# Copying each row in 16 column blocks, one for each DMA engine, with the first 128 columns apart

## The chip, the cores and the metric

One core of a Trainium2 chip. The metric is the device time of one execution in microseconds (us); lower is better. GB/s in the profiles is what the copies moved one way; read plus written is twice that. A run counts as "slow" here if it is over 1.5% above the fastest run of the same kernel, and verdicts use the other runs ("fast") alone. Several chips of the same kind were used, so a kernel is compared with the kernel before *on the same chip*; absolute times from different jobs are not compared.

## The reference

```python
def setup_inputs():
    return {"x": np.random.randn(8192, 8192).astype(np.float32), "shift": 100}

def reference(x, shift):
    return np.roll(x, shift, axis=1)
```

Each row of 8,192 floats (32 KiB) is rotated right by 100 columns (400 B). Nothing is computed. 268 MB are read and 268 MB written.

## The kernel before

```python
    s = shift % n_cols                      # 100
    engines = [nc.sync, nc.scalar]          # two queues that issue transfers
    n_chunks = 16
    rows_per_chunk = n_rows // n_chunks     # 512

    for i in range(n_chunks):
        r0 = i * rows_per_chunk
        r1 = r0 + rows_per_chunk
        eng = engines[i % 2]
        eng.dma_start(out=out[r0:r1, s:], in_=x[r0:r1, : n_cols - s])    # the wide copy
        eng.dma_start(out=out[r0:r1, :s], in_=x[r0:r1, n_cols - s:])     # the narrow copy
# ... launch code cut
```

Every copy goes from HBM to HBM, with no stop on the core. Below, "wide copy" and "narrow copy" are the two kinds marked here; a "packet" is one contiguous run of bytes, as the trace records it.

## Time and profile before

| | before |
|---|---|
| time, 3 runs | 850.75 us (848.87 to 853.41) |
| span of the profile | 830.1 us |
| packets of 32,368 B (wide) | 8,192, mean 1,568 ns, fastest tenth 1,199 ns |
| packets of 400 B (narrow) | 8,192, mean 35 ns, median 24 ns |

The profiled execution was about 20 us shorter than the three timed ones. In the other runs below, the span is only about 2 us under the time of the same run, and this kernel took 836 to 842 us on other chips. So this profile seems to come from a faster chip, and a difference between it and another profile has to be taken with that in mind.

From the page of the kernel before: the span; the mean busy share of the 16 DMA engines in 40 equal slices of the span, in tenths; what they moved in each slice; packet counts; the two queues with packets, MB and share of the 16 engines' span; and HBM traffic.

```profile
span 830.1 us, 77 instructions
...
DMA  9999999999999999999999999999999999999996
GB/s 306 324 326 315 328 322 323 331 329 328 334 323 334 338 311 340 324 334 334 306 339 324 332 329 314 328 331 335 329 305 335 332 328 326 311 334 328 329 326 208
DMA packets 16896, 268.44 MB, mean 323 GB/s; under 512 B 8704, under 2 KB 8704, under 8 KB 8704
...
q1 hardware_dynamic: 8448, 134.22, 49.8%
q10 hardware_dynamic: 8448, 134.22, 49.1%
HBM read 268.44 MB, written 268.44 MB: 647 GB/s over the span
```

The engines are busy in every slice but the last. 49.8% and 49.1% for the two queues mean that packets fill nearly all of the engines' time. The HBM line (HBM is the chip's main memory) is the limit to look at: 647 GB/s of reads and writes. The Trainium skill (HBM Reference, Specifications) gives about 716 GB/s for the memory that two cores share; the trace is at 90% of that. That the memory is what limits the kernel is the reading that fits.

The next lines are the order of issues around the end of a chunk: start, duration (both us), the queue, line, operation, and how many were merged. L33 is the wide copy, L34 the narrow one.

```profile
start us, us, engine line op out<-in xcount [idle before <-releaser]
311.49 0.51 SPq L33 DMA_DIRECT2D out_dram<-in_x_dram  x1
313.59 0.52 ACTq L33 DMA_DIRECT2D out_dram<-in_x_dram  x1
315.96 94.76 SPq L34 DMA_DIRECT2D out_dram<-in_x_dram  x1
317.51 93.26 ACTq L34 DMA_DIRECT2D out_dram<-in_x_dram  x1
```

A wide copy is issued in 0.5 us. The narrow copy behind it is held up for 93 to 95 us, because the queue takes no more for the time being; by then the next wide copy is already in the queue. The same place in a table of windows (window in us, POOL, clock, busy share of the DMA engines, GB/s); 300 to 320 us is where the narrow packets run:

```profile
core 0: us, POOL busy (x), PEclk, DMA share, GB/s
250.00:300.00 50.00, 0.00 (x0) 1.00 0.99 333
300.00:320.00 20.00, 0.00 (x0) 1.00 0.99 307
320.00:370.00 50.00, 0.00 (x0) 1.00 1.00 334
```

The engines stay busy there, at 307 in place of 333 GB/s.

### The profile page before, as it was taken

The page shows a single profiled execution, that of the slowest core. Times are in us where ns is not written, and L with a number is a line of the kernel's source. Part 1 is how long each engine was busy: PE and PEld are TensorE (multiplying, and loading weights), DVE is VectorE, ACT ScalarE, POOL GpSimd, SP SyncE. Part 2 cuts the span into 40 slices and gives each one's busy share as a digit, 9 for nine tenths or more (in the row PEclk, how much of TensorE's full clock was granted, in tenths as well). Part 3 has the DMA queues.
Part 4 walks back from the last instruction along what each step waited for, and adds up shares of the span by engine and source line. Part 5 has one row for each costly group of instructions (what it writes and reads, how often), then busy time and mean ns, then how long its engine had stood idle before and what let it go on. Part 6 is the DMA issues. An engine that isn't in the chain of part 4 may idle for free. (4 is left out here: it accounts for less than half of the span.)

```text
span 830.1 us, 77 instructions
## 1 busy us (share of the span) xinstructions
POOL 0.2 (0%) x4
## 2 busy tenths in 40 slices
POOL 0000000000000000000000000000000000000000
DMA  9999999999999999999999999999999999999996
GB/s 306 324 326 315 328 322 323 331 329 328 334 323 334 338 311 340 324 334 334 306 339 324 332 329 314 328 331 335 329 305 335 332 328 326 311 334 328 329 326 208
DMA packets 16896, 268.44 MB, mean 323 GB/s; under 512 B 8704, under 2 KB 8704, under 8 KB 8704
## 3 DMA queue, kind: packets, MB, share of 16 engines
q1 hardware_dynamic: 8448, 134.22, 49.8%
q10 hardware_dynamic: 8448, 134.22, 49.1%
HBM read 268.44 MB, written 268.44 MB: 647 GB/s over the span
## 5 line engine op out<-in xcount | busy, mean ns | idle before, releaser
L51 POOL MEMSET const-bfloat16-1.0<- 128x1 bf16 x1 | 0.1, 102 | 0.0
L51 POOL MEMSET const-uint8-127<- 128x1 uint8 x1 | 0.1, 102 | 0.0
L51 POOL MEMSET const-float32-0.0<- 128x1 f32 x1 | 0.1, 99 | 0.2 <-issue 0.2
L51 POOL MEMSET const-float32-1.0<- 128x1 f32 x1 | 0.1, 99 | 0.0
## 6 DMA issues: line engine op xcount, KB each, us to landing
out_dram<-in_x_dram SPq DMA_DIRECT2D x8, 16184.0 KB, 206.1
out_dram<-in_x_dram ACTq DMA_DIRECT2D x8, 16184.0 KB, 206.3
out_dram<-in_x_dram ACTq DMA_DIRECT2D x8, 200.0 KB, 205.8
out_dram<-in_x_dram SPq DMA_DIRECT2D x8, 200.0 KB, 205.6
```

The lines of the kernel that those rows point to most:

```text
L51: nc = _bacc.Bacc("TRN2", target_bir_lowering=False, num_devices=1)
```

## The change

The intent: give each of the 16 DMA engines its own sixteenth of every row, begin the blocks at a destination column that is a multiple of 128 (512 B), and copy the first 128 destination columns apart.

```diff
     s = shift % n_cols
+    a = -(-s // 128) * 128
...
     for i in range(n_chunks):
-        r0 = i * rows_per_chunk
-        r1 = r0 + rows_per_chunk
         eng = engines[i % 2]
-        eng.dma_start(out=out[r0:r1, s:], in_=x[r0:r1, : n_cols - s])
-        eng.dma_start(out=out[r0:r1, :s], in_=x[r0:r1, n_cols - s:])
+        r = slice(i * rows, (i + 1) * rows)
+        if a < n_cols:
+            eng.dma_start(
+                out=out[r, a:].rearrange("r (e w) -> e r w", e=16),
+                in_=x[r, a - s:n_cols - s].rearrange("r (e w) -> e r w", e=16),
+            )
+        for d, c, n in [(0, n_cols - s, s), (s, 0, a - s)]:
+            if n > 0:
+                eng.dma_start(out=out[r, d:d + n], in_=x[r, c:c + n])
```

With a shift of 100, `a` is 128, a block is (8192 - 128) / 16 = 504 columns = 2,016 B, and there are two narrow copies, of 100 and of 28 columns (400 and 112 B).

More of the change, by code (lines that the diff above doesn't have):

```diff
@@ L21 @@
     s = shift % n_cols
+    a = -(-s // 128) * 128
     engines = [nc.sync, nc.scalar]
     n_chunks = 16
-    rows_per_chunk = n_rows // n_chunks
+    rows = n_rows // n_chunks
     for i in range(n_chunks):
-        r0 = i * rows_per_chunk
-        r1 = r0 + rows_per_chunk
         eng = engines[i % 2]
-        eng.dma_start(out=out[r0:r1, s:], in_=x[r0:r1, : n_cols - s])
-        eng.dma_start(out=out[r0:r1, :s], in_=x[r0:r1, n_cols - s:])
+        r = slice(i * rows, (i + 1) * rows)
[7 more added lines that the diff above has]
+                eng.dma_start(out=out[r, d:d + n], in_=x[r, c:c + n])
 _INS = ['x', 'shift']
```

## The prediction

> **What bounds the kernel now.** Nothing computes; the page's DMA row stands at 9 tenths in every slice but the last, and the two queues' packets take 49.8% + 49.1% of 16 engines' span of 830.1 us. The packet records split that: 8,192 packets of 32,368 B (mean 1,568 ns, 803 us shared by 16 engines), 8,192 of 400 B (mean 35 ns, 18 us), semaphore packets of 9 ns. The large ones are not at the engine's own speed: a tenth take 1,199 ns (27 B/ns), the mean is 20.6 B/ns. At 1,199 ns all would need 614 us, so 190 us go on waiting for something the engines share. The page's HBM line, 647 GB/s read plus written, points to the memory: the Trainium skill (HBM Reference, Specifications) gives about 716 GB/s for the domain, and the trace is at 90% of it. Little is left to gain. Issues take 0.5 to 0.9 us, no limit.
>
> **What the change does.** The bytes stay, and both forms use 16 engines (skill, DMA: Bandwidth & Descriptors, how many engines k: the outermost dimension, before 512 rows, now 16 blocks). An engine got 32 whole rows of a chunk; now one column block of all 512: 131,072 packets of 2,016 B, each 32 KiB after the last. 8,192 packets of 112 B (columns 100 to 127) are added; the 400 B ones stay.
>
> - Engine time: 4 B take 9 ns, 400 B 24 ns, 32,368 B 1,199 ns at best: about 9 ns + 1 ns per 27 B, so 84 ns for 2,016 B; over 16 engines some 700 us against 614. Under 803, so most of it hides behind the memory, not all: 12% of the large packets already run at engine speed.
> - Memory: 2,016 is no multiple of 64 or 256, so nearly every block starts and ends inside a 256 B unit on both sides; the aligned start helps only the first block. I estimate 3 to 6% more memory work and poorer locality than 32 KiB runs. Large copies: 803 -> about 835 us.
> - 112 B packets: estimated 20 to 25 ns from the 400 B ones, so 10 to 13 us, all critical, as every engine is always busy.
> - Neighbouring blocks written together in place of 16 streams 1 MiB apart: may lower memory conflicts; I give it little.
> - 16 more issues, 256 more semaphore packets: under 1 us. Descriptor supply: about 1,000 packets of 400 B passed in one 5 us window, 200 per us; the change needs some 160: no starvation, though not by much.
>
> **Prediction.** 851 + 32 + 11 gives about 890 us, range 835 to 970. Faster by over 2%: 0.13; within 2%: 0.20; slower by over 2%: 0.67.
>
> **What would show it.** Right: the DMA row still 9, 2,016 B packets at a mean of 100 to 105 ns (98 is today's rate), minimum 80 to 87; 112 B packets 20 to 35 ns; HBM 600 to 630 GB/s. Wrong in size: a mean at the minimum (engines bound, no longer memory), or far above 110 (the memory dislikes 32 KiB steps). DMA share well under 90%: descriptors arrive too slowly.
>
> **What would make it wrong.** If today's loss is conflicts between streams 1 MiB apart, neighbouring blocks could run near the engine floor and give 760 to 820 us. If each engine keeps hitting the same few memory channels[...], it could pass 1,000 us.

## The result, and the profile after

The changed kernel took 936.48 us in the median of 4 runs (920.90 to 947.59), two of them slow; the kernel before took 851.7 us beside it. The ratio is 1.087 (95% interval 1.080 to 1.093): slower. A ratio here and below is the mean time of one kernel's fast runs over that of the other's in the same rounds, so it is not quite the ratio of the medians. On another chip the same kernel came out at 1.056 (below); the size of the loss differed between the two chips, its sign did not.

The same parts of the page, for the changed kernel (a fast run of 929.29 us):

```profile
span 927.5 us, 93 instructions
...
DMA  9999999996999977999879999999989999999995
GB/s 279 320 320 314 237 303 319 322 317 201 263 303 304 308 222 232 317 322 316 251 216 304 317 317 287 264 318 320 319 248 287 322 310 318 251 307 312 315 315 162
DMA packets 148224, 268.44 MB, mean 289 GB/s; under 512 B 17152, under 2 KB 148224, under 8 KB 148224
...
q1 hardware_dynamic: 74112, 134.22, 48.9%
q10 hardware_dynamic: 74112, 134.22, 48.5%
HBM read 268.44 MB, written 268.44 MB: 579 GB/s over the span
```

There are now 148,224 packets in place of 16,896. Two things differ. Between the dips the rate is 315 to 320 GB/s, formerly 325 to 335. And about every 115 us there is a dip to 200 to 265 GB/s, in some of which the engines' busy share falls to 6, 7 or 8 tenths. Before, the row of nines had no gap.

Around the dip near 340 us, the order of issues (L31 wide, L37 narrow) and the windows:

```profile
start us, us, engine line op out<-in xcount [idle before <-releaser]
233.08 107.60 SPq L37 DMA_DIRECT2D out_dram<-in_x_dram  x2
235.95 108.49 ACTq L37 DMA_DIRECT2D out_dram<-in_x_dram  x2
340.73 11.74 SPq L31 DMA_DIRECT2D out_dram<-in_x_dram  x1
344.48 10.17 ACTq L31 DMA_DIRECT2D out_dram<-in_x_dram  x1
356.28 102.03 SPq L37 DMA_DIRECT2D out_dram<-in_x_dram  x1
359.29 102.77 ACTq L37 DMA_DIRECT2D out_dram<-in_x_dram  x1
```

```profile
core 0: us, POOL busy (x), PEclk, DMA share, GB/s
250.00:320.00 70.00, 0.00 (x0) 1.00 1.03 299
325.00:360.00 35.00, 0.00 (x0) 1.00 0.68 204
370.00:440.00 70.00, 0.00 (x0) 1.00 1.02 318
```

The wide copies of the next chunk are issued at 340.73 and 344.48 us, *behind* the narrow ones and in the middle of the dip, and take 10 to 12 us where before they took 0.5. From 325 to 360 us the engines are only 68% busy. (Shares over 1, as 1.03 here, come from packet records that overlap.)

Three measures are used from here on. They are worked out from the trace's packet records, or from the completions of copies, each of which is signalled once by each of the 16 engines:

- *full rate*: mean GB/s of those 2 us windows in which at least 15.5 engines are busy and no narrow packet runs;
- *idle*: time that engines have no packet, in us, summed over the engines and divided by 16. Each 1 us stretch counts as at most 16 busy engines. Packet records overlap, with 2,016 B packets in about 40% of the time, so this is rather too small, and it depends on the stretch: for the changed kernel 43 us with stretches of 5 us and 55 with 1 ns, for the kernel before 6 and 10;
- *drift*: time from the first to the last of the 16 completions of one wide copy, mean over a run's wide copies. (Both kernels show 16 for each, as the Trainium skill has it: DMA: Bandwidth & Descriptors, Why a DMA increments its semaphore by 16 and not by 1.)

A packet record does not name its engine or its address. Which rows or blocks an engine has, here and below, follows from the form of the copies and was not seen in a trace.

| | before | after | difference |
|---|---|---|---|
| first packet to last | 827 us | 924 us | +97 |
| full rate | 331.2 GB/s | 314.3 GB/s | |
| the wide copies' bytes at the full rate | 801 us | 841 us | +40 |
| idle | 10 us | 48 us | +38 |
| rest (narrow packets, start, end) | 16 us | 35 us | +19 |
| drift | 8.5 us | 20.5 us | |

If the kernel before ran in this chip's 851 us and not in its profile's some 832, its whole trace would be longer by the factor 1.023, and the first difference some 20 us in place of 40 (an estimate from these numbers). That leaves 78 us, near the 74 that the ratio gives (0.0867 x 851.7). So 39% (38 of 97) to 49% (38 of 78) of the loss is not a lower rate but engines without work.

### The profile page after: what moved, and what is told of

Same layout as the page of the kernel before. It is cut to its first block, busy times and chain, and to the rows that moved or that the text cites. A ratio compares the mean times of both kernels' runs of the same rounds, so it can differ in the third digit from the quotient of the medians.

```text
span 927.5 us, 93 instructions
## 1 busy us (share of the span) xinstructions
POOL 0.2 (0%) x4
## 2 busy tenths in 40 slices
DMA packets 148224, 268.44 MB, mean 289 GB/s; under 512 B 17152, under 2 KB 148224, under 8 KB 148224
```

## The experiments

Theory A, at first: the wide copies are a few per cent slower for their 2,016 B packets, and the rest is lost where one copy hands over to the next. Few packets lie ahead in a queue, so narrow copies between wide ones let the engines run dry. Rivals: the narrow packets themselves are dear (R1); or the column blocks finish at different times, with or without narrow copies (R2).

In the first job the changed kernel itself was not run, so its figures there stand beside 1.087, which was measured on another chip; since 1.056 and 1.087 both occur, differences of 0.03 between jobs say nothing by themselves.

All in one table; "full rate", "idle" and "drift" are of the profiled run. The profiles of big_only and after_again2 fell in slow runs, so for these only the ratio (fast runs) is used in an argument.

| run | what it is | ratio to before (95%) | full rate | idle | drift |
|---|---|---|---|---|---|
| *first job* | | | | | |
| smalls_last | after, narrow copies at the end | 1.110 (1.100 to 1.119) | 320.3 | 65 | 33 |
| big_only | after, no narrow copies | 1.044 (1.037 to 1.052) | 315.4 (slow) | 57 (slow) | 31 (slow) |
| four_chunks | after, 4 chunks | 1.088 (1.079 to 1.097) | 319.4 | 49 | 49 |
| rows_2016 | 2,016 B packets, engines have whole rows | 1.082 (1.075 to 1.089) | 314.6 | 26 | 18 |
| *second job* | | | | | |
| after_again2 | after | 1.056 (1.047 to 1.065) | 321.7 (slow) | 34 (slow) | 19 (slow) |
| blocks_1792b | blocks with equal offsets | 1.058 (1.049 to 1.067) | 318.5 | 33 | 25 |
| rows_from_128b | before, split at column 128 | 1.018 (1.012 to 1.024) | 331.4 | 7 | 7 |
| flip_act2 | before, narrow first on one queue | 0.997 (0.989 to 1.004) | none | 16 | 13 |
| *third job* | | | | | |
| rows_4032 | rows, 4,032 B packets | 1.131 (1.123 to 1.138) | 309.2 | 30 | 16 |
| rows_8064 | rows, 8,064 B packets | 1.024 (1.020 to 1.029) | 335.6 | 13 | 5 |
| rows_2016_four | rows_2016 in 4 chunks | 1.089 (1.082 to 1.096) | 322.7 | 55 | 39 |
| blocks_2048 | aligned blocks of 2,048 B, no shift | 0.999 (0.992 to 1.007) | 328.1 | 11 | 12 |

The kernel before took 836.29, 841.52 and 835.91 us in the three jobs (medians of 7 runs).

### smalls_last: the narrow copies moved to the end

```diff
+    for i in range(n_chunks):
+        eng = engines[i % 2]
+        r = slice(i * rows, (i + 1) * rows)
         for d, c, n in [(0, n_cols - s, s), (s, 0, a - s)]:
```

> The changed kernel with the same copies, but the narrow ones (100 and 28 columns) issued after all the wide ones. Theory A (the loss at the end of each chunk is a hand-over loss: few packets lie ahead in a queue, so with the narrow copies between two wide ones the next wide one is handed out only when the last engine is done with the one before): the eight dips go, the 25 us of narrow packets stand once at the end, span 840 + 25 + start, 865 to 890 us, ratio to before 1.02 to 1.05. Rival R1 (the narrow packets themselves are what costs the 63 us, wherever they stand): 920 to 940 us, and a tail of some 60 us.

Measured: 1.110, no better than the 1.087 of the change itself (on another chip) and far from the 1.02 to 1.05 of theory A, which fell in this form. From its page, busy tenths and GB/s:

```profile
DMA  9999999999999999979999599994999989998297
GB/s 287 320 323 324 325 324 324 318 324 312 315 318 323 316 316 324 324 235 305 327 328 315 186 303 325 325 322 143 309 325 326 316 258 317 323 326 272 74 83 61
```

and windows between two dips, in one, behind it, and at the end:

```profile
core 0: us, POOL busy (x), PEclk, DMA share, GB/s
430.00:500.00 70.00, 0.00 (x0) 1.00 1.03 324
505.00:540.00 35.00, 0.00 (x0) 1.00 0.71 221
545.00:610.00 65.00, 0.00 (x0) 1.00 1.03 322
860.00:932.00 72.00, 0.00 (x0) 1.00 0.64 73
```

Two losses can be told apart. The dips are there without any narrow copy near them. The first 400 us have none: the completions of the first five wide copies on one queue are spread over 7, 21, 29, 39 and 47 us, so the engines drift apart by some 10 us per 100 us until the fast ones run dry (505 to 540 us: 71% busy). That is R2. And the narrow packets, alone at the end, fill 64 us of windows at a mean of 76 GB/s: R1 is right in that narrow packets with no wide ones beside them are dear (400 B ones took a mean of 58 ns here, 32 in the changed kernel).

The issues show how a dip comes about. The issue of a wide copy returns when the *slowest* engine has about 100 packets of the copy before left: for the fifth, 22.3 us before its last completion, which at 512 packets in 114.6 us is 100 packets; the other copies of both queues give 95 to 123 (an estimate, as the engine's rate within a copy isn't seen). By then the fastest engine had completed its part of that copy 25 us ago. The reading that fits is that the next copy's packets are laid out for the 16 engines only when those of the copy before are. The Trainium skill (DMA: Bandwidth & Descriptors, Queues, rings and completion order) says that a copy is split over one ring on each engine; it does not say how far ahead a ring is filled. No run here changed that depth by itself, so this hand-over is read from the trace, not tested.

### big_only: the wide copies alone (wrong)

```diff
-        for d, c, n in [(0, n_cols - s, s), (s, 0, a - s)]:
-            if n > 0:
-                eng.dma_start(out=out[r, d:d + n], in_=x[r, c:c + n])
```

> The changed kernel without the narrow copies; the first 128 columns stay unwritten, so the result is wrong on purpose. Shows the wide copies alone, 16 boundaries included. Theory A: no dips, as a wide copy follows a wide one directly: 2,016 B packets at 314 GB/s, 845 to 865 us. Rival R2 (the dips come from the switch of the wide copy to another region, or from column blocks that finish at different times, with or without narrow copies): dips stay, 880 to 910 us.

Measured: 1.044, fast runs 869 to 879 us. The absolute figures lie between the two expectations, and as they were written for a slower chip the run decides by its ratio: the wide copies alone, with 1.6% fewer bytes than the kernel before, lose 4.4%. Its profile is of a slow run and is left aside; that dips need no narrow copies is seen in smalls_last.

### four_chunks: a quarter of the boundaries

```diff
-    n_chunks = 16
+    n_chunks = 4
```

> The changed kernel in 4 chunks of 2,048 rows in place of 16 of 512: the same packets, a quarter of the boundaries. Theory A: of 63 us lost at 8 pairs of boundaries about 25 us (engine time of the narrow packets) stays, and the rest shrinks to a quarter: 880 to 900 us. Rival R1 (cost of the narrow packets themselves): as the changed kernel, 920 to 940 us.

Measured: 1.088, beside 1.087 for the changed kernel (another chip), and idle time 49 us as there (48). The absolute time, 905 to 918 us in fast runs, lies between the two expectations, which were written for a slower chip. No saving from fewer boundaries is seen: the drift of one copy is 49 us in place of 20. The reading that fits is that what is lost at a boundary is the drift collected since the last one: engines with equal shares and unequal speed, and a boundary that only collects it.

### rows_2016: the same packets, but whole rows on each engine

```diff
-            eng.dma_start(
-                out=out[r, a:].rearrange("r (e w) -> e r w", e=16),
-                in_=x[r, a - s:n_cols - s].rearrange("r (e w) -> e r w", e=16),
-            )
+            dst = out[r, a:].rearrange("r (e t w) -> t r e w", e=8, t=2)
+            src = x[r, a - s:n_cols - s].rearrange("r (e t w) -> t r e w", e=8, t=2)
+            for t in range(2):
+                eng.dma_start(out=dst[t], in_=src[t])
```

The even blocks and the odd ones are copied apart, so that the runs stay 2,016 B long.

> The changed kernel's 2,016 B packets and narrow copies, but the engines get whole rows again (32 rows each, first the even blocks, then the odd ones, in two copies). If the drop of the steady rate from 329 to 314 GB/s is the packet's size, the steady rate is again 310 to 318 GB/s; if it is the column block (32 KiB steps on each engine, same columns always) it is back at 325 to 332 GB/s. Theory A expects dips like the changed kernel's, as the packets ahead are as small; a rival that blames column blocks which end at different times expects none.

Measured: 1.082, full rate 314.6 GB/s, as the changed kernel's 314.3 (on another chip). So the lower rate does not need column blocks: it goes with this cut of the row. Drift and idle time are smaller here (18 and 26 us), but this kernel also has two wide copies per chunk, which rows_2016_four sorts out.

### rows_2016_four: the same in 4 chunks

Relative to rows_2016:

```diff
-    n_chunks = 16
+    n_chunks = 4
```

> rows_2016 in 4 chunks of 2,048 rows, so an engine passes over all columns in 128 rows and is handed new work a quarter as often. In four_chunks (column blocks) the 16 completions of a wide copy lay 37 to 61 us apart. If fixed columns on an engine make the engines unequal: completions within 15 us, idle under 20 us. If engines are unequal with small packets whatever their addresses: 30 to 60 us apart and idle 30 to 50 us.

Measured: 1.089, drift 39 us (up to 56), idle 55 us. From its page:

```profile
DMA  9999999999999999997799999999899999999563
GB/s 269 328 322 324 321 324 320 326 311 300 325 326 322 326 324 318 324 308 132 79 309 320 325 322 320 327 323 319 290 305 323 327 323 325 323 325 325 208 148 33
...
HBM read 268.44 MB, written 268.44 MB: 588 GB/s over the span
```

Each engine passes over all columns, and the engines drift apart as they do with column blocks. That rules out the fixed columns as a necessary cause of the drift.

### blocks_1792b: all blocks at the same offset

In the changed kernel the blocks' starts lie at eight different offsets in a 256 B unit, as 2,016 is 32 short of 2,048. The Trainium skill (DMA: Bandwidth & Descriptors, How a descriptor splits into AXI transactions) says that a transfer is cut into pieces that start at 256 B boundaries, so that bytes in front of an unaligned start are fetched for nothing. This case's trace agrees only in that the packet times of 2,016 B stand in clusters: 43% at 81 or 82 ns and smaller ones at 88 (9%) and 93 ns (10%). If one engine always has the dearest block, it must fall behind.

```diff
-    a = -(-s // 128) * 128
+    a = n_cols - 16 * 448
```

> Column blocks of 448 columns (1,792 B, seven times 256 B) from column 1,024 on, so that all 16 blocks begin at the same offset in a 256 B unit (source 112, destination 0); columns 100 to 1,023 are copied by rows (3,696 B). Correct result. Theory A2 (the engines drift apart because each always has the same block, and blocks lie at different offsets: packet times cluster at 82, 88, 93 and 99 ns): one cluster is left, the 16 completions of a wide copy lie within 10 us in place of 16 to 40, idle time falls below 25 us, ratio 1.03 to 1.06 in spite of more packets per byte. Rival A3 (the drift comes from memory channels behind fixed columns, whatever the offset): spread and idle time stay, ratio 1.08 or more.

Measured: 1.058, the same as the changed kernel in this job (1.056). One cluster is left, as expected: 83% of the 1,792 B packets took 73 or 74 ns. But drift (25 us for the block copies) and idle time (33 us) stay. So theory A2 fell: *different* offsets on the engines are not what makes them unequal. The source is still unaligned here for every block, by 112 B. Yet 74 ns is no more than the aligned packets of blocks_2048 (below) lead one to expect: with 9 ns for a 4 B packet and 84 ns for 2,048 B, 1,792 B should take about 75 ns (an estimate). So the price of an unaligned start that the page tells of is not seen in most packets' times; with 2,016 B too the largest cluster, 82 ns, is under 84. 8,192 row pieces of 3,696 B with unaligned starts at the destination were added, so the run does not tell which of these keeps up the loss.

### after_again2: the change on the second job's chip

No edit.

> The changed kernel itself, so that the others of this job have it on the same chip. Ratio to before as on record, 1.08 to 1.10; 16 engines' worth of idle time 40 to 55 us, as in its first trace.

Measured: 1.056, below the 1.087, with disjoint intervals. The expectation missed: the chip matters. Only the second job's kernels are compared with this figure.

### rows_from_128b: only the split at column 128

```diff
-        eng.dma_start(out=out[r0:r1, s:], in_=x[r0:r1, : n_cols - s])
+        eng.dma_start(out=out[r0:r1, 128:], in_=x[r0:r1, 128 - s:n_cols - s])
         eng.dma_start(out=out[r0:r1, :s], in_=x[r0:r1, n_cols - s:])
+        eng.dma_start(out=out[r0:r1, s:128], in_=x[r0:r1, :128 - s])
```

> The kernel before, with only the split at column 128 taken over: rows of 32,256 B with an aligned destination, and the 112 B copies. The 112 B packets took 8 us of 16 engines in the changed kernel. If that is all they cost: ratio 1.005 to 1.015. If narrow copies between wide ones cost by themselves what the changed kernel lost (63 us for both kinds): 1.03 or more. If the aligned destination helps: below 1.00.

Measured: 1.018, 15 us (0.018 x 841.5), a little over the expected range. The full rate is 331.4 GB/s, the same as the 331.2 before (the two profiles are from different chips): no gain from the aligned destination is seen with long packets. The 112 B packets took 14 us of the 16 engines here, and the 400 B ones 21 in place of 18.

### flip_act2: narrow phases of the two queues apart

```diff
-        eng.dma_start(out=out[r0:r1, s:], in_=x[r0:r1, : n_cols - s])
-        eng.dma_start(out=out[r0:r1, :s], in_=x[r0:r1, n_cols - s:])
+        copies = [(s, 0, n_cols - s), (0, n_cols - s, s)]
+        for d, c, n in copies if i % 2 == 0 else copies[::-1]:
+            eng.dma_start(out=out[r0:r1, d:d + n], in_=x[r0:r1, c:c + n])
```

> The kernel before, with the narrow copy issued ahead of the wide one on the second queue, so that the two queues' narrow phases no longer coincide and each runs beside wide packets of the other queue. The windows with narrow packets took 96 us at a mean of 271 GB/s, against 331 without. If narrow packets cost only where all engines do them at once, up to 17 us are gained: ratio 0.98 to 0.99. If the engine time of narrow packets can't be hidden: 0.995 to 1.005.

Measured: 0.997 (0.989 to 1.004), the same. The dips of the narrow phases are gone from its profile, but idle time is 16 us and drift 13, with completions of the last wide copies up to 19 us apart. A gain of 0.5% is within the interval; the 17 us hoped for are not there. This was the one try at a version better than the kernel before, and it isn't one that could be told apart from it.

### rows_4032 and rows_8064: longer packets

Relative to rows_2016:

```diff
-            dst = out[r, a:].rearrange("r (e t w) -> t r e w", e=8, t=2)
+            dst = out[r, a:].rearrange("r (e t w) -> t r e w", e=4, t=2)    # rows_4032; e=2 in rows_8064
...                                                                          # the same for src
```

> As rows_2016 (whole rows on each engine, the changed kernel's narrow copies), but with 4,032 B packets. Theory A (what a queue holds ahead is counted in packets, some 100 of them on an engine; the engines are not equally fast, and one that is further ahead than those packets last has nothing to do): twice the bytes ahead, so idle time falls from 26 us (rows_2016) to 10 to 15, and the fixed part of each packet halves: ratio 1.03 to 1.05. If the loss were the aligned start, the narrow copies or the number of copies, which are those of rows_2016, it would stay at 1.08.

> The same with 8,064 B packets. Theory A: 100 packets are now some 80 us of work ahead, more than the engines drift apart; idle under 10 us, rate with all engines busy 327 to 332 GB/s, ratio 1.018 to 1.03, close to rows_from_128, which has the same narrow copies and 32,256 B packets (1.018).

Measured for 8,064 B: 1.024, full rate 335.6 GB/s, drift 5 us, idle 13 us; the expected range for the ratio, a little over for idle. What is left of the loss is about what rows_from_128b has, with the same narrow copies.

Measured for 4,032 B: 1.131, the slowest of all, and a plain miss. Its page:

```profile
DMA  8999999999999999999999999999999999899996
GB/s 251 324 262 330 258 285 320 263 323 241 302 328 254 327 226 311 326 262 327 214 319 313 270 332 213 297 303 267 329 222 307 301 267 330 216 286 292 278 331 169
```

The engines are busy nearly throughout, and still slices of about 325 GB/s stand beside others of 210 to 300. 4,032 B packets with a median of 156 ns took a mean of 218. So there is a loss that is not idle time, and that no theory here foresaw.

Smaller windows of the same trace show where it sits. From 70 to 100 us, with both queues on the odd blocks, 327 GB/s are moved; from 56 to 66 us, when the first queue has gone on to odd blocks and the second still copies even ones, 200 GB/s with all engines busy; and from 107 to 123 us, where the narrow copies run, 163. Over the run's eight changes from even to odd (the stretch between the two queues' last even completions) the mean rate is 246 GB/s, with rows_2016 287 and with rows_8064 334. The 2 us windows with narrow packets add up to 260 us at 234 GB/s, against 98 us at 277 in the kernel before. So both losses lie where one copy hands over to the next; why they are largest with 4,032 B stays open.

### blocks_2048: column blocks with aligned ends (wrong)

```diff
             eng.dma_start(
-                out=out[r, a:].rearrange("r (e w) -> e r w", e=16),
-                in_=x[r, a - s:n_cols - s].rearrange("r (e w) -> e r w", e=16),
+                out=out[r, :].rearrange("r (e w) -> e r w", e=16),
+                in_=x[r, :].rearrange("r (e w) -> e r w", e=16),
             )
```

Relative to big_only. It copies without the shift, so the result is wrong, but it moves the same bytes as the kernel before, in as many short packets as big_only: 16 column blocks, one for each engine.

> As big_only, but 16 blocks of 512 columns, copied without a shift (wrong on purpose), so that every packet of 2,048 B begins on a 256 B boundary on both sides. big_only had 315 GB/s with all engines busy and 57 us idle, ratio 1.044. If misaligned ends cost the memory what was predicted (3 to 6%): 325 to 332 GB/s; if the packet's fixed time is the cause of the lower rate: 313 to 320 GB/s. If the offsets make the engines unequal: idle under 25 us; else again 40 to 60.

Measured: 0.999, against 1.044 for big_only. Its page:

```profile
DMA  9999999999999999999999999999999999999995
GB/s 288 328 325 316 324 333 327 329 326 329 323 330 324 337 325 332 329 329 330 324 332 327 329 329 328 331 326 331 329 329 332 326 325 328 335 323 324 322 320 187
...
HBM read 268.44 MB, written 268.44 MB: 646 GB/s over the span
```

The row of nines has no gap, the rate is 328 GB/s, idle time 11 us, drift 12 us (up to 26 in the last copies), and the memory is back at 646 GB/s. 131,072 packets of 2 KiB in column blocks are thus as fast as 8,192 rows with the narrow copies beside them. 85% of the packets took 84 ns. The packets' number, their length of about 2 KiB and the column blocks are thus not enough for what the change lost. What blocks_2048 took away is two things at once: the ends off the 256 B boundaries, and the 400 B between a packet's place in the source row and in the destination row. The first is the likelier cause, as longer packets with the same shift keep the full rate (335.6 GB/s in rows_8064), but no run has short aligned packets with the shift, so the second is a rival that stands untested. Also, big_only ran on another chip. On this chip misaligned 2,016 B packets were dear too: rows_2016_four is at 1.089, rows_8064 with the same narrow copies at 1.024. Beside rows_2016_four the full rate of blocks_2048 differs little (328.1 against 322.7), idle time much (11 against 55 us).

## Why the prediction was right or wrong

The direction was right (given a chance of 0.67), and 936.48 lies within 835 to 970, but above the 890 in the middle. That it lies within owes something to the width of the range, as a term of 38 us was left out of the sum, and the size was partly the chip's: 890 over 851 is 1.046, and the two chips gave 1.056 and 1.087. Of the signs that the prediction named, the fastest 2,016 B packet (80 ns) came as foretold; their mean (107 ns for 100 to 105), the 112 B packets (mean 16 ns for 20 to 35), the HBM rate (579 GB/s for 600 to 630) and the DMA row (slices of 6 to 8) did not. Point by point:

- *Memory-bound, little to gain.* Right as far as it was tried: no correct version was measurably faster, and no run moved more than 647 GB/s. What the engines share and wait for was not isolated.
- *"Large copies: 803 -> about 835 us"*, from 3 to 6% more memory work at misaligned ends. The full rate fell by 5% (331.2 to 314.3) between the two profiles, some 3% if the faster chip of the first is allowed for. The size came out about right, +40 or +20 against +32, but the 3 to 6% had been worked out from nothing, so that is in part luck; on one chip, rows_2016_four against blocks_2048, the rate differs by 1.7% alone, some 13 us. The cause fits: with aligned ends and no shift the column blocks lost nothing (0.999 against 1.044). The engine floor of 84 ns was right too (82 to 84 at the fastest clusters), and it did hide behind the memory.
- *"112 B packets: ... 10 to 13 us"*. In the changed kernel these packets took 8 us of engine time, but the split alone, in the form with rows, cost 15 us (1.018). Slightly too small: in that run the 112 B packets took 14 us and the 400 B ones beside them 21 in place of 18.
- *The step that failed* is "as every engine is always busy", with "the DMA row still 9" and "no starvation, though not by much". The term for idle engines stood at 0 in the sum and measured +38 us (10 to 48). The supply of packets was never too slow on the whole: between dips all 16 engines are at work. The reading that fits is that it was too slow for the engines that were *ahead*. With misaligned 2 KiB packets the engines drift apart by 20 us in a copy (8.5 before), and what lies ahead of an engine seems to be counted in packets, some 100 (read from smalls_last, not tested); before, two wide copies were in a queue at a time. 38 us is nearly what lies between 890 and the fast runs' 925.
- *"If each engine keeps hitting the same few memory channels"*: not what was seen. Fixed columns are neither needed for the loss (rows_2016_four has it) nor enough for it (blocks_2048 hasn't).

What is shown: cut into 2,016 B packets, with misaligned ends and shifted, the wide copies alone lose 4.4%, by a lower rate and by idle engines, which aligned and unshifted ones do not (0.999, on another chip); and the split with its extra narrow copy costs about 2%. Together that is 6.3% (4.5 + 1.8, though big_only moves 1.6% fewer bytes than blocks_2048), against 5.6% and 8.7% on the two chips. What is only read from traces: the hand-over of a copy to all engines at a time. What is open: whether it is the misaligned ends or the shift between source and destination; why engines become *unequal* (equal offsets did not cure it); whether source or destination matters more, as blocks_2048 aligned both; and rows_4032. With a shift of 400 B, source and destination can't both be on 256 B boundaries in a plain copy, so blocks_2048 is a measurement and not a way out; long packets, as in the kernel before, make such ends rare.

## What to carry to other kernels

When a memory-bound copy must be cut into short runs, align both ends of each run if the data allow it; if they don't, keep the runs long. Here 2 KiB runs were free when they began at multiples of 2,048 B on both sides and were not shifted, and cost 4 to 5% otherwise; which smaller unit would do was not tried. "Long" is no rule without a measurement either: 8,064 B cost 2.4% with the narrow copies, 4,032 B 13%. And a mean busy share of 97% can hide two fifths to a half of a loss: look at the slices for dips, and at how far apart the engines' completions of one copy lie, before putting a loss down to bandwidth.

## What the Trainium skill lacked or had wrong

- DMA: Bandwidth & Descriptors, Queues, rings and completion order: no figure for how far ahead a ring is filled. In smalls_last the issue of a copy of 512 packets per engine was held up until the slowest engine had some 100 packets of the copy before left (estimates of 95 to 123), while others were idle: 49 to 65 us of idle time in smalls_last, four_chunks and rows_2016_four.
- The same page, How a descriptor splits into AXI transactions: gives the extra pieces of an unaligned start. The packet times agree in part only: clusters at 82, 88 and 93 ns for 2,016 B, but 82 ns for the largest and 74 ns for 1,792 B that all start 112 B off at the source, no more than 84 ns for 85% of the aligned 2,048 B packets lead one to expect. It says nothing of the larger effect seen here, engines drifting apart: 20 us within one wide copy in the changed kernel and 49 in four_chunks, against 12 with aligned ends and no shift (blocks_2048).
- The same page, Bandwidth: its table is for HBM to SBUF, the core's own memory, and has no figure for copies from HBM to HBM. (Latency and other measured facts has one, 207 to 214 GB/s per direction at best, for tiles of a large row pitch.) The runs show at most 331 to 336 GB/s each way with all engines busy, 647 GB/s read and written over a span.
- HBM Reference, Specifications: about 716 GB/s for the domain; no run came over 647, with one core at work and as much written as read. The page has no figure for such a mix; whether the memory sets the 647 was not tested.
- No page explains rows_4032: 4,032 B packets of whole rows at 1.131, while 2,016 B (1.082, on another chip) and 8,064 B (1.024) are faster.
